# Two attention units of the last token tile are scored amid the last input columns, whose token halves are reordered

## The chip, the cores and the metric

The kernel runs on one core of one Trainium2 chip. The metric is the device time of one execution in microseconds (us), lower is better. The core has a matrix engine (PE; its weight loads are listed apart as PEld), a vector engine (DVE), a scalar engine (ACT), a general one (POOL), and queues that issue transfers between device memory (DRAM) and on-chip memory; nearly all transfers here are issued by the queue of SP. Each engine runs its own list of instructions in a fixed order and waits where an instruction's inputs, or the buffer it writes, are not ready. PSUM is the small memory that PE writes, in eight banks of 128 x 512 f32 numbers.

## The reference

One layer of a hybrid decoder, for a prompt of 1024 tokens and for 8 sample tokens of one step each:

```
h    = rms_norm(x) ;  p = h @ w_in                  # 1024 -> 3480 columns
q, rows4, rows_w, gates = NSA part of p             # 8 query heads, 2 key/value heads, width 64
o_nsa = gates . (compressed, causal/selected, window-of-512 attention)
o_rw  = RWKV-7 recurrence on the u columns of p
o_mem = attention of 4 more query heads over 256 memory tokens, keys and values from mem @ w_mem_kv
y = x + concat(o_nsa*silu(z_nsa), o_rw*silu(z_rw), o_mem*silu(z_mem)) @ w_out
```

With 1024 tokens there are 16 selectable blocks, and 16 are selected, so for the prompt the "selected" branch is causal attention over all earlier keys. The sample tokens run the same layer against cached pages. All rows, states and memory keys and values are returned too.

## The kernel before, in words

**Precision.** Products run on PE in a 4-byte format that keeps part of the mantissa, so an operand x is split into a high part (ACT copies it with rounding) and a low part (DVE or POOL subtracts), and a product is three matmuls: high·high, low·high, high·low. For the attention scores a 64-wide query is laid with its low part in the other 64 rows ("qhl", turned by PE into `p_q` and copied to `qs`), and the keys exist as `kh` and `kl`.

**Phase 1** (`phase1`) normalises x, transposes it into tiles `h` (high and low, 16 for each half of the tokens; H = 0 holds tokens 0 to 511 and the samples, H = 1 tokens 512 to 1023) in the pool `hp`, and walks over `w_in` in blocks of 128 columns. For a block, `wblock` loads 512 KB (`wraw`, SP), ACT makes `whi` and DVE `wlo`; `project` emits 24 matmuls per piece of tokens into `p_pr`: two pieces of 264 and 256 for H = 0, one of 512 for H = 1; a `do_...` function then evicts. For the gate columns `do_z` runs tanh on ACT and a multiply on DVE into the tile `zt`, and SP writes it to the DRAM buffer `z_d`. The RWKV recurrence is interleaved with the first 17 column blocks. The last four blocks (`cols[EARLY:]`, all gate columns) are emitted by `columns`: block by block, H = 0, then H = 1. While they run, a background generator `ahead` is stepped, `BG` steps for every 8 steps of the projection: it makes the compressed keys (`prompt_cmp`), the memory keys and values (`mem_kv`, matmuls into `p_mo`), the stacked keys (`attn_keys`, `p_k`), and the queries of tile 7 (`q_stack(7)`).

**Phase 2** (`phase2`) runs attention by tiles of 128 tokens, from tile 7 down to 0, in units of (tile, key/value head, pair of query heads), four to a tile. Of a unit, `attn_scores` makes four score blocks: PE writes `p_s` (two banks), DVE adds the mask, finds the minimum and evicts to `p`, ACT takes the exponential (L1357), POOL scales `p` by the gate and the inverse sum (L1382). `attn_turn` transposes `p` by PE into `p_pT` in groups of four 128 x 128 pieces, which ACT and DVE copy to `pt` in turn, and `attn_out` multiplies with the values into `p_o` and then with the gate columns in `cat`, which `load_z` reads back from `z_d`. The class `InOrder` holds PE to the written order. Side tasks are drawn by `slot` between these pieces: `query_tasks` brings the compressed branch of a tile (`attn_cmp`: scores `p_sc`, softmax `pcq`, four transposes) and the queries of the next (`q_stack(6)`: load `q` from the DRAM buffer `q_d`, ACT and POOL make `qhl`, PE transposes it to `p_q`), and other generators the sample tokens' and memory work. `until(0, ("cmp", i))` runs steps of `query_tasks` until tile i's compressed branch stands. The phase begins with six pieces of the scores of units 0 and 1, a slot after each.

**Order.** A tile of a pool reuses the memory of an earlier one, and the scheduler makes its first writer wait for the earlier one's last user. Pools of phase 2 lie over memory of phase 1. That is how a transfer of phase 2 can have to wait for an eviction of phase 1.

**Phase 3** projects `cat` by `w_out`, adds x, and finishes the sample tokens.

Of the kernel before, what the change touches and what calls it, by code (L numbers as in the profile page):

```python
# [10 lines left out]
F32 = mybir.dt.float32  # L11
# [10 lines left out]
NS = 8  # L22
# [3 lines left out]
PTB = 8  # L26
KB = 2
FREE = 0
ORDER = [4, 1, 11, 2, 3, 6, 5, 7, 13, 17, 10, 9, 15, 8, 0, 12, 14, 18, 16, 19, 20]
EARLY = 17  # L30
BG = 6
STEP = 0.7
# [16 lines left out]
def bc(ap, shape):  # L49
    return ap.to_broadcast(shape)  # L50
# [64 lines left out]
class Step:  # L115
# [130 lines left out]
    def h_tiles(self, H, k):  # L246
        W = HALF + (NS if H == 0 else 0)
        return [self.hp.tile([128, W], F32R, name=f"h{p}{H}_{k}") for p in range(2)]

# [201 lines left out]
    def phase1(self):  # L451
# [8 lines left out]
        with ExitStack() as ctx:  # L460
            P = lambda name, bufs, **k: ctx.enter_context(tc.tile_pool(name=name, bufs=bufs, reuse_waits="tile", **k))
            self.small = P("small", 2)
            self.hp = P("hp", 1)
            self.ev = P("ev", 1)
            self.wr = P("wr", 2)
            self.wp = P("wp", 2)
            rctx = ctx.enter_context(ExitStack())
            PR = lambda name, bufs: rctx.enter_context(tc.tile_pool(name=name, bufs=bufs, reuse_waits="tile"))
# [7 lines left out]
            self.ptr = P("ptr", 2, space=PSUM)  # L476
            self.pw = P("pw", 3, space=PSUM)
            self.hi, self.lo = ([], []), ([], [])
# [131 lines left out]
    def columns(self, tiles):  # L610

        rest = None
        for c0, do, j in tiles:
            m = 24 if j is None else 128
            hi, lo = self.wblock(c0, m)
            for H in range(2):
                out = []
                self.open = True
                for k, n in enumerate(self.project(H, hi, lo, m, out)):
                    if k < 7:  # L620
                        yield n
# [459 lines left out]
    def mem_kv(self):  # L1081
# [15 lines left out]
        for k in range(0, 8, 2):  # L1097
            raw = self.wr.tile([128, 2, 512], F32, name="wraw")
            nc.sync.dma_start(raw[:], I["w_mem_kv"][0, k * 128:(k + 2) * 128, :].rearrange("(k p) c -> p k c", p=128))
            wh = self.wp.tile([128, 2, 512], F32R, name="whi")  # L1100
            wl = self.wp.tile([128, 2, 512], F32R, name="wlo")
            A.activation(wh[:], raw[:], AF.Copy)
            V.tensor_tensor(wl[:], raw[:], wh[:].bitcast(F32), op=OP.subtract)
            yield
            for j in range(2):
                for t in range(2):
                    cs = slice(t * 128, (t + 1) * 128)
                    h, l = his[k // 4][:, (k + j) % 4, cs], los[k // 4][:, (k + j) % 4, cs]
# [4 lines left out]
        for t in range(2):  # L1113
            d0 = bass.AP(tensor=dst.tensor, offset=dst.offset + t * 128 * 512, ap=[[512, 128], [1, 512]])
            mv = self.slot(2 + t, [128, 256], F32, f"mv{t}")
            A.activation(mv[:], po[t][:, 256:512], AF.Copy)
            kn = self.norm_rope(po[t][:, 0:256].rearrange("p (t c) -> p t c", t=1), 5, 1, 4, None)
            nc.sync.dma_start(d0[:, 0:256], kn.rearrange("p h d -> p (h d)"))
            nc.sync.dma_start(d0[:, 256:512], mv[:])
            yield  # L1120

# [151 lines left out]
    def attn_cmp(self, i):  # L1273

        nc = self.nc
        V, A, G, PE = nc.vector, nc.scalar, nc.gpsimd, self.te
# [6 lines left out]
        for j in range(4):  # L1283
# [3 lines left out]
            if j == 1:  # L1287
                yield 0.1
        pcq = self.we.tile([128, 8, 64], F32, name="pcq", tag="pcq")
        v3 = lambda x: x.rearrange("p a b c -> p (a b) c")  # L1290
# [12 lines left out]
        V.tensor_tensor(gh, gh, gate[:, :, 0].rearrange("p (g h) -> p g h", g=2), op=OP.mult)  # L1303
        (G if i < 7 else V).tensor_tensor(pcq[:], pcq[:], bc(rc[:, :, None], [128, 8, 64]), op=OP.mult)
        yield 7.0 if i < 7 else 4.0
        self.pcT[i] = self.pt_copy(lambda j: pcq[:, 2 * j:2 * j + 2, :].rearrange("p a b -> p (a b)"), "c")
        yield

# [23 lines left out]
    def attn_scores(self, i, g, hp, Ps):  # L1332
# [28 lines left out]
        for b in range(2):  # L1361
# [3 lines left out]
            if split:  # L1365
                for h in range(2):
                    ps = self.pS.tile([128, 1024], F32, name="p_s", tag="s")
# [101 lines left out]
    def query_tasks(self):  # L1469

        yield from self.attn_cmp(7)
        self.done.add(("cmp", 7))
# [39 lines left out]
    def phase2(self):  # L1512
        tc, nc, I, O = self.tc, self.nc, self.I, self.O
        with ExitStack() as ctx:
            P = lambda name, bufs, **k: ctx.enter_context(tc.tile_pool(name=name, bufs=bufs, reuse_waits="tile", **k))
            self.small = P("small2", 2)
            self.we = P("we", 1)
            self.wk = P("wk", 1)
            self.tk = self.wk
# [3 lines left out]
            self.pM = Tag(self.pT, "t")  # L1523
            self.pp = P("pp", 4)
            self.load_z(7)
# [9 lines left out]
            P = [{} for _ in units]  # L1535
            self.done, self.tail, self.jobs, self.unit = set(), [], [], 0
# [96 lines left out]
    def sample_tables(self):  # L1633
# [11 lines left out]
        V.tensor_scalar(t[:, 4:7, :, 0], t[:, 4:7, :, 0], -1.0, None, op0=OP.mult)  # L1645
        return rows[:NS, 0:896].rearrange("p (k c) -> p k c", k=7)

    def sample_setup(self):
# [11 lines left out]
        for x in (qb, q64, qmb, self.gr):  # L1660
            G.memset(x[:], 0.0)
        sums = self.slot(1, [128, 1024], F32, "s_in1")[:, 0:128]
        nc.sync.dma_start(sums, I["c_rw"][:, 128:256])
        rows = self.sample_tables()

# [768 lines left out]
```

## Time and profile before

| What | us |
|---|---|
| three timed executions | 963.06, 966.33, 966.30 (median 966.3) |
| the profiled execution, its own time | 963.45 |
| its span (what the profile covers) | 961.7 |
| PE busy in the span | 923.5 (96%) |
| DVE, ACT, POOL busy | 653.2, 442.0, 179.5 |
| TensorE clock granted, mean | 0.998 |

Phase 1 ends, as PE sees it, with the last `p_pr` at 513.25 us; the compressed keys, memory keys and last columns fill about 436 to 513. Phase 2 starts behind it. In the timelines a row is a run of like instructions with the start, the duration, the line, the engine, output and inputs, and in brackets how long the engine stood idle before it and what ended that. In a table of stretches each engine's busy time stands with its number of instructions, then the granted clock (1.00 is full speed), the DMA engines' busy share and GB/s.

### The profile page before, as it was taken

The numbers are of one execution on the slowest core, as the hardware profiler recorded it, in microseconds if no ns is written. First come the engines' busy times: TensorE is split into PE (matmuls) and PEld (weight loads), VectorE is DVE, ScalarE is ACT, GpSimd is POOL, SyncE is SP. The second block draws the span as 40 slices with busy tenths as digits, with TensorE's granted clock in tenths as the row PEclk, the third lists the DMA queues.
The fourth block names the chain that finished last, engine by engine and source line by source line (L and its number), as shares of the span: only waits on it lengthen the run. The fifth ranks groups of instructions, "written<-read, shape, count | busy, mean of one in ns | idle before, by whom it ended". The sixth has DMA issues, their size and how long they took to land.

```text
span 961.7 us, 24727 instructions
## 1 busy us (share of the span) xinstructions
PE 923.5 (96%) x9845; PEld 785.5 (82%) x9845; DVE 653.2 (68%) x2025; ACT 442.0 (46%) x990; POOL 179.5 (19%) x270
## 2 busy tenths in 40 slices
PE   8999999999999998999998899999999998999997
PEld 8998888868898886788976787888888887887975
DVE  6668579846593798653447876756678996548474
ACT  7664324332432342222434666566576766324321
POOL 2000000000000000000001444354354665102010
PEclk9999999999999999999999999999999999999999
DMA  7521304312331127145426624240210035977721
GB/s 272 132 67 35 100 14 131 89 47 56 88 100 37 35 54 193 46 105 151 107 88 183 184 68 151 76 140 24 69 40 9 9 111 164 333 246 212 235 74 40
DMA packets 133964, 103.82 MB, mean 108 GB/s; under 512 B 34705, under 2 KB 121240, under 8 KB 133720
## 3 DMA queue, kind: packets, MB, share of 16 engines
q1 hardware_dynamic: 128888, 90.53, 32.5%
q0 software_dynamic: 3200, 10.49, 3.1%
q8 instruction: 78, 1.28, 0.5%
q10 hardware_dynamic: 1760, 1.21, 0.4%
q14 instruction: 38, 0.31, 0.1%
HBM read 83.61 MB, written 22.78 MB: 111 GB/s over the span
## 4 chain that ended last, share of the span: by engine, by line
PE 70%; DVE 16%; ACT 6%; DMA 4%; issue 3%; SPq 1%; POOL 0%; DVEq 0%; ACTq 0%; POOLq 0%
PE p_pr L87 20%; PE p_out L87 9%; PE p_pr L307 6%; PE p_s L87 5%; PE p_pT L87 4%; PE p_o L87 4%; PE p_hid L87 3%; ACT p L1357 2%; DVE p L1356 2%; PE p_iy L87 2%; PE p_z L87 1%; PE p_it L87 1%; PE p_sc L87 1%; DVE pt L1329 1%; DVE wlo L284 1%
## 5 line engine op out<-in xcount | busy, mean ns | idle before, releaser
L87 PE MATMUL p_pr<-h,whi 128*128 128x512 f32 (+5 forms) x1024 | 248.4, 335 | 0.0
L87 PEld LDWEIGHTS p_pr<-h,whi 128*128 128x128 f32 (+1 forms) x1024 | 161.8, 184 | 18.9 <-issue 2.8
L87 PE MATMUL p_pr<-h,wlo 128*128 128x512 f32 (+5 forms) x512 | 164.7, 325 | 0.6 <-DVE wlo L284 0.6
L1382 POOL TENSOR_SCALAR p<-p,fac,gates 128x640 f32<-128x640 f32 (+7 forms) x128 | 104.2, 825 | 106.1 <-DVE fac L1379 62.2
L1357 ACT ACTIVATE p<-p,nm 128x640 f32<-128x640 f32 (+7 forms) x128 | 93.0, 728 | 54.1 <-DVE nm L1356 47.6
L87 PEld LDWEIGHTS p_pr<-h,wlo 128*128 128x128 f32 (+1 forms) x512 | 93.6, 184 | 10.4 <-DVE wlo L284 0.8
L87 PE MATMUL p_pT<-ident,p 128*128 128x128 f32 x528 | 70.8, 279 | 5.7 <-ACT pt L1327 2.2
L1031 POOL MEMSET w2d<- 128x128 f32 x1 | 0.2, 206 | 393.6 <-PE p_yy L87 393.6
L1356 DVE CUSTOM_DVE_ANT_0 p<-p_s,bmask 128x512 f32<-128x512 f32 (+7 forms) x96 | 60.3, 662 | 18.4 <-PE p_s L87 16.6
L87 PEld LDWEIGHTS p_pT<-ident,p 128*128 128x128 f32 x528 | 56.7, 140 | 16.6 <-issue 6.4
L87 PE MATMUL p_s<-kh,qs 128*128 128x512 f32 (+3 forms) x191 | 66.3, 359 | 2.8 <-DVE nm L1356 2.8
L307 PE MATMUL p_pr<-h,whi 128*128 128x264 f32 (+2 forms) x320 | 68.6, 309 | 0.3 <-ACT whi L283 0.3
L87 PE MATMUL p_o<-pt,vs 128*64 128x128 f32 x1056 | 67.9, 277 | 0.4 <-DVE cat L1415 0.4
L284 DVE TENSOR_TENSOR wlo<-wraw,whi 128x1024 fp32r<-128x1024 f32 (+1 forms) x34 | 40.7, 1197 | 38.1 <-ACT whi L283 38.1
L87 PEld LDWEIGHTS p_o<-pt,vs 128*64 128x64 f32 x1056 | 57.0, 137 | 7.2 <-issue 3.8
L87 PE MATMUL p_s<-kl,qs 128*128 128x512 f32 (+3 forms) x192 | 61.0, 338 | 0.0
L283 ACT ACTIVATE whi<-wraw 128x1024 fp32r<-128x1024 f32 (+1 forms) x35 | 36.4, 1039 | 50.0 <-PE p_pr L87 35.7
L1329 DVE COPY pt<-p_pT 128x512 f32<-128x512 f32 (+1 forms) x72 | 48.3, 674 | 13.6 <-PE p_pT L87 12.8
L307 PEld LDWEIGHTS p_pr<-h,whi 128*128 128x128 f32 x320 | 51.1, 189 | 3.3 <-ACT whi L283 0.8
L87 PE MATMUL p_out<-woh,chi 128*128 128x512 f32 x128 | 51.7, 404 | 0.0
L87 PE MATMUL p_out<-woh,clo 128*128 128x512 f32 x128 | 50.2, 392 | 0.4 <-DVE clo L2267 0.4
L87 PE MATMUL p_out<-wol,chi 128*128 128x512 f32 x128 | 49.9, 390 | 0.0
(549 smaller groups left out, 1931.2 us busy)
## 6 DMA issues: line engine op xcount, KB each, us to landing
wraw<-in_w_in_dram SPq DMA_DIRECT2D x34, 512.0 KB, 4.0
pg<-in_c_pool_dram SPq DMA_DIRECT2D x32, 256.0 KB, 6.5
pg<-in_c_pool_dram SPq DMA_DIRECT2D x48, 128.0 KB, 2.2
x<-in_x_prompt_dram SPq DMA_DIRECT2D x8, 512.0 KB, 7.3
z_d<-zt SPq DMA_DIRECT2D x16, 256.0 KB, 2.2
cat<-z_d SPq DMA_DIRECT2D x8, 512.0 KB, 5.9
xres<-in_x_prompt_dram POOLq DMA_DIRECT2D x16, 256.0 KB, 3.9
out_dram<-xres POOLq DMA_DIRECT2D x16, 256.0 KB, 3.6
```

What stands on the lines that cost most here:

```text
L87: self.last = getattr(self.engine, op)(*a, **k)
L283: nc.scalar.activation(hi[:, :, :n], raw[:, :, :n], AF.Copy)
L284: (low or nc.vector).tensor_tensor(lo[:, :, :n], raw[:, :, :n], hi[:, :, :n].bitcast(F32), op=OP.subtract)
L307: self.last_mm = self.pe.matmul(ps[:m, :b - a], w[:, k, :m], h[k][:, a:b], start=(k == 0 and i == 0), stop=(k == 7 and i == 2))
L1031: nc.gpsimd.memset(w2d[:], 0.0)
L1329: nc.vector.tensor_copy(pt[:, :n], ps[:, :n])
L1356: V.tensor_tensor_reduce(halves(x), halves(ps), m, -1.0, 3.0e38, op0=OP.add, op1=OP.min, accum_out=nm[:, h, b:b + 1])
L1357: A.activation(x, x, AF.Exp, scale=-1.0, bias=nm[:, h, b:b + 1], accum_out=sm[:, h, b:b + 1])
L1382: nc.gpsimd.tensor_scalar(x, x, f[:, h, b:b + 1], gate[:, hd + h, 1 + b:2 + b], op0=OP.mult, op1=OP.mult)
```

## The change

Four things are moved, and no matmul is added or taken away.

1. `halves` takes the place of `columns` for the last four blocks: all four for H = 0, then all four for H = 1. Each block's weights are loaded and split once for each half, so four loads of 512 KB, four `whi` and four `wlo` are added. The eviction follows its projection at once. `BG` is 9 instead of 6.
2. When the four of H = 0 are through, the `h` tiles of half 0 (their pool is now a separate one, `hp0`), the three PSUM banks `pw`, and the pool `wk1` are freed. Over the first is laid the pool `pp` of the probabilities `p`, which before was opened in phase 2; two of the banks become `p7`, one score buffer. The background generator then goes on to `scores`, which emits `attn_scores` of the first two units of tile 7 amid the columns of H = 1. Phase 2 starts without scores of its own for these units, with two slots instead of six.
3. The compressed branch of tile 7 is split: its scores and softmax (`cmp_weights`) go into the background work of phase 1 (`stacked`), and the four transposes (`cmp_turn`) stay at the start of phase 2. Its last multiply is on POOL; before it was on DVE for tile 7. The constant tables of the sample tokens go into phase 1 too.
4. `mem_kv` copies both halves of `p_mo` to one tile, normalises the keys of both together and writes them with one transfer, where before each half had its own chain and two writes.

```diff
@@ phase1
-            self.hp = P("hp", 1)
+            hp1 = P("hp1", 1)
...
+            self.hp = hctx.enter_context(tc.tile_pool(name="hp0", ...)), hp1
...
-            self.wk = self.tk = P("wk1", 1)
+            self.wk = self.tk = wctx.enter_context(tc.tile_pool(name="wk1", bufs=1, reuse_waits="tile"))
             self.pM = Tag(self.ptr, "tr")
-            bg = self.ahead()
-            late = self.columns(cols[EARLY:])
+            def scores():
+                while len(self.half) < len(cols[EARLY:]):
+                    yield
+                pctx.close()
+                wctx.close()
+                hctx.close()
+                self.p7 = P("p7", 1, space=PSUM)
+                self.pp = self.kctx.enter_context(tc.tile_pool(name="pp", bufs=4, reuse_waits="tile", side="right"))
+                for n in range(UNITS):
+                    yield from self.attn_scores(7, 0, n, self.begun[n])
+                self.p7 = None
+
+            self.begun, self.half = [{} for _ in range(UNITS)], []
+            bg = chain(self.ahead(), scores())
+            late = self.halves(cols[EARLY:])
             for _ in group(late, 8):
                 for _ in islice(bg, BG):
                     pass
@@ ahead
+        def stacked():
+            while 7 not in self.qs:
+                yield
+            self.pc7 = self.slot(3, [128, 8, 64], F32, "pcq")
+            yield from self.cmp_weights(7, self.pc7)
+            self.tables = self.sample_tables()
-        yield from weave(chain(self.prompt_cmp(), self.mem_kv()), keys())
+        yield from weave(chain(self.prompt_cmp(), stacked(), self.mem_kv()), keys())
+    def halves(self, tiles):
+        for H in range(2):
+            for c0, do, j in tiles:
+                out = []
+                yield from self.project(H, *self.wblock(c0, 128), 128, out)
+                do(H, out, j)
+                self.half.append(H)
@@ mem_kv
+        m = self.slot(6, [128, 2, 512], F32, "mrows")
+        for t in range(2):
+            A.activation(m[:, t], po[t][:], AF.Copy)
...
@@ query_tasks
-        yield from self.attn_cmp(7)
+        yield from self.cmp_turn(7, self.pc7)
@@ phase2
+            self.wk = P("wk", 1)
             self.we = P("we", 1)
-            self.wk = P("wk", 1)
...
-            self.pp = P("pp", 4)
...
-            start = chain(scores(0), scores(1))
-            for k in range(6):
-                next(start)
+            start = chain(*(scores(n) for n in range(UNITS, 2)))
+            for k in range(2):
+                next(start, None)
                 slot()
```

**PE, amid the columns.** In the lists below a row is a line, an operation, output and inputs, and the shape; `kh` and `kl` are the keys, `qs` the queries. PE in the kernel before, at the end of the last column:

```order
L307 MATMUL p_pr<-h_7_913,whi 128x512
L307 MATMUL p_pr<-h_7_914,whi 128x512
L307 MATMUL p_pr<-h_7_913,wlo 128x512
L84 MATMUL p_s<-kh_6300,qs 128x512
L87 MATMUL p_s<-kl_6301,qs 128x512
L87 MATMUL p_s<-kh_6303,qs 128x512
L87 MATMUL p_s<-kl_6304,qs 128x512
L87 MATMUL p_sc<-cmask 128x512
```

PE in the changed kernel, in the second half's columns (line numbers are higher by one for the same helper):

```order
L308 MATMUL p_pr<-h_1_674,whi 128x512
L1395 MATMUL p_s<-kh_6303,qs 128x128
L1396 MATMUL p_s<-kl_6304,qs 128x128
L1395 MATMUL p_s<-kh_6306,qs 128x512
L1396 MATMUL p_s<-kl_6307,qs 128x512
L308 MATMUL p_pr<-h_1_673,wlo 128x512
```

The scores that followed the last column, all of them in a row, stand in groups of four between projections.

**PE, where the queries of tile 6 are turned.** Before, in the first part of phase 2:

```order
L87 MATMUL p_sn<-ident,s_in_7259 128x8 x7
L87 MATMUL p_pT<-ident,pcq 128x128 x4
L87 MATMUL p_s<-kh_6300,qs 128x128
L87 MATMUL p_s<-kl_6301,qs 128x128
L87 MATMUL p_s<-kh_6303,qs 128x512
L87 MATMUL p_s<-kl_6304,qs 128x512
L87 MATMUL p_q<-ident,qhl 128x128 x4
```

Now, at the border of the two phases (the last `p_pr` of all is the third row):

```order
L308 MATMUL p_pr<-h_7_916,whi 128x512
L308 MATMUL p_pr<-h_7_917,whi 128x512
L308 MATMUL p_pr<-h_7_916,wlo 128x512
L88 MATMUL p_pT<-ident,p 128x128 x8
L88 MATMUL p_q<-ident,qhl 128x128 x4
L88 MATMUL p_pT<-ident,p 128x128 x10
L88 MATMUL p_s<-kh_6303,qs 128x512
```

Before, 53 rows lay between the last `p_pr` and the first `p_q` of tile 6; now one row of eight transposes does.

**SP, the load of those queries.** The queue's order before:

```order
L1118 DMA out_dram<-nr_y 128x256
L320 DMA z_d<-zt 128x512
L1129 DMA kd<-out_dram 128x4x64
L1254 DMA q<-q_d 128x768
L1129 DMA kd<-out_dram 128x4x64
L1254 DMA q<-q_d 128x768
```

and now:

```order
L1171 DMA mv<-out_dram 128x256
L321 DMA z_d<-zt 128x512
L1824 DMA mxv_8132<-in_cache_mem_dram 128x2x256 x2
L321 DMA z_d<-zt 128x512
L1295 DMA q<-q_d 128x768 x2
L1311 DMA y_rw<-y_d 128x256
L1312 DMA cat_7335<-z_d 128x8x128
```

The last `z_d` row is the write of the very last column's gates in both. The loads of `q` stand right behind it now. The memory of the first `q` tile lies over the `zt` tile that this write reads, so the load also waits until the write has landed.

More of the change, by code (lines that the diff above doesn't have):

```diff
@@ L27 @@
 KB = 2
+UNITS = 2
 FREE = 0
@@ L30 @@
 EARLY = 17
-BG = 6
+BG = 9
 STEP = 0.7
@@ L247, in h_tiles @@
         W = HALF + (NS if H == 0 else 0)
-        return [self.hp.tile([128, W], F32R, name=f"h{p}{H}_{k}") for p in range(2)]
+        return [self.hp[H].tile([128, W], F32R, name=f"h{p}{H}_{k}") for p in range(2)]
     def turn_hs(self):
@@ L466, in phase1 @@
             self.wp = P("wp", 2)
+            hctx = ctx.enter_context(ExitStack())
+            self.hp = hctx.enter_context(tc.tile_pool(name="hp0", bufs=1, reuse_waits="tile")), hp1
             rctx = ctx.enter_context(ExitStack())
@@ L476, in phase1 @@
             self.ptr = P("ptr", 2, space=PSUM)
-            self.pw = P("pw", 3, space=PSUM)
+            pctx = ctx.enter_context(ExitStack())
+            self.pw = pctx.enter_context(tc.tile_pool(name="pw", bufs=3, reuse_waits="tile", space=PSUM))
             self.hi, self.lo = ([], []), ([], [])
@@ L555, in phase1 @@
             self.key_pools()
-            self.wk = self.tk = P("wk1", 1)
+            wctx = ctx.enter_context(ExitStack())
+            self.wk = self.tk = wctx.enter_context(tc.tile_pool(name="wk1", bufs=1, reuse_waits="tile"))
             self.pM = Tag(self.ptr, "tr")
-            bg = self.ahead()
-            late = self.columns(cols[EARLY:])
+            def scores():
[12 more added lines that the diff above has]
+            late = self.halves(cols[EARLY:])
             for _ in group(late, 8):
@@ L1111, in mem_kv @@
             yield
-        dst = O["mem_kv_prompt"]
[L1113 to L1120, printed above, removed]
+        m = self.slot(6, [128, 2, 512], F32, "mrows")
+        for t in range(2):
+            A.activation(m[:, t], po[t][:], AF.Copy)
+        y = m[:, :, 0:256].rearrange("p t (h d) -> p t h d", d=64)
+        sq = self.slot(7, [128, 8, 64], F32, "nr_sq")
+        A.activation(sq[:].rearrange("p (t h) d -> p t h d", t=2), y, AF.Square)
+        ss = self.small.tile([128, 8], F32, name="nr_ss", tag="nrss8")
+        V.tensor_reduce(ss[:], sq[:], axis=AX.X, op=OP.add)
+        r = self.rsqrt(self.small, ss[:], 8, 1.0 / 64, 1e-6)
+        yield
+        V.tensor_tensor(y, y, bc(r.rearrange("p (t h) -> p t h", t=2)[:, :, :, None], [128, 2, 4, 64]), op=OP.mult)
+        V.tensor_tensor(y, y, bc(self.gains[:, 5:6, None, :], [128, 2, 4, 64]), op=OP.mult)
+        dst = O["mem_kv_prompt"]
+        nc.sync.dma_start(bass.AP(tensor=dst.tensor, offset=dst.offset, ap=[[512, 128], [128 * 512, 2], [1, 512]]), m[:])
+        yield
     def mem_keys(self):
@@ L1273, in attn_cmp, with cmp_turn, cmp_weights @@
     def attn_cmp(self, i):
+        pcq = self.we.tile([128, 8, 64], F32, name="pcq", tag="pcq")
+        yield from self.cmp_weights(i, pcq)
+        yield 7.0
+        yield from self.cmp_turn(i, pcq)
+    def cmp_turn(self, i, pcq):
+        self.pcT[i] = self.pt_copy(lambda j: pcq[:, 2 * j:2 * j + 2, :].rearrange("p a b -> p (a b)"), "c")
+        yield
+    def cmp_weights(self, i, pcq):
         nc = self.nc
@@ L1288, in attn_cmp @@
                 yield 0.1
-        pcq = self.we.tile([128, 8, 64], F32, name="pcq", tag="pcq")
         v3 = lambda x: x.rearrange("p a b c -> p (a b) c")
@@ L1303, in attn_cmp @@
         V.tensor_tensor(gh, gh, gate[:, :, 0].rearrange("p (g h) -> p g h", g=2), op=OP.mult)
[L1304 to L1307, printed above, removed]
+        G.tensor_tensor(pcq[:], pcq[:], bc(rc[:, :, None], [128, 8, 64]), op=OP.mult)
     def attn_rwkv(self, i):
@@ L1366, in attn_scores @@
                 for h in range(2):
-                    ps = self.pS.tile([128, 1024], F32, name="p_s", tag="s")
+                    ps = (self.p7 or self.pS).tile([128, 1024], F32, name="p_s", tag="s")
                     scores(ps[:, c0:512], qs[:, hd + h, :], b, c0, 512)
@@ L1534, in phase2 @@
                 groups += [(n, a, min(a + size, total)) for a in range(0, total, size)]
-            P = [{} for _ in units]
+            P = self.begun + [{} for _ in units[UNITS:]]
             self.done, self.tail, self.jobs, self.unit = set(), [], [], 0
@@ L1645, in sample_tables @@
         V.tensor_scalar(t[:, 4:7, :, 0], t[:, 4:7, :, 0], -1.0, None, op0=OP.mult)
-        return rows[:NS, 0:896].rearrange("p (k c) -> p k c", k=7)
+        self.nc.sync.dma_start(rows[:, 896:1024], self.I["c_rw"][:, 128:256])
+        return rows[:NS, 0:896].rearrange("p (k c) -> p k c", k=7), rows[:, 896:1024]
     def sample_setup(self):
@@ L1661, in sample_setup @@
             G.memset(x[:], 0.0)
-        sums = self.slot(1, [128, 1024], F32, "s_in1")[:, 0:128]
-        nc.sync.dma_start(sums, I["c_rw"][:, 128:256])
-        rows = self.sample_tables()
+        rows, sums = self.tables
         x, sq, xr = (self.we.tile([128, 8, NS], F32, name=f"s_x{k}") for k in range(3))
```

## The prediction

> **What bounds the kernel now.** I read the page's busy shares and chain first, then tables of stretches around the end of phase 1, PE's waits there, and the timelines of each engine.
>
> ```profile
> PE 923.5 (96%) x9845; PEld 785.5 (82%) x9845; DVE 653.2 (68%) x2025; ACT 442.0 (46%) x990; POOL 179.5 (19%) x270
> PE 70%; DVE 16%; ACT 6%; DMA 4%; issue 3%; SPq 1%; POOL 0%; DVEq 0%; ACTq 0%; POOLq 0%
> ```
>
> PE is busy for 923.5 of 961.7 us, and it holds 70% of the chain that ended last. The change gives PE the same work, so the time can move only through PE's idle time, 38.2 us in all, and through the clock. The stretches that the change touches:
>
> ```profile
> 436.00:513.00 77.00, 75.29 (x484) 64.12 (x483) 32.86 (x92) 29.67 (x60) 3.26 (x6) 1.00 0.40 111
> 513.00:540.00 27.00, 21.35 (x147) 17.04 (x145) 23.56 (x76) 15.64 (x33) 10.87 (x11) 0.94 0.82 241
> 540.00:600.00 60.00, 57.07 (x582) 47.45 (x581) 39.85 (x105) 40.62 (x100) 26.12 (x30) 1.00 0.35 110
> ```
>
> (Columns: stretch, length, then busy time of PE, PEld, DVE, ACT, POOL, the granted clock, DMA share, GB/s.) The last columns leave PE idle for 77.00 - 75.29 = 1.7 us, the border of the phases for 27.00 - 21.35 = 5.65 us, the 60 us behind it for 2.9 us. Inside the border:
>
> ```profile
> 517.50:520.00 2.50, 0.01 (x1) 0.01 (x1) 2.06 (x5) 0.03 (x1) 0.00 (x0) 1.00 0.45 95
> 520.00:522.00 2.00, 2.00 (x7) 1.38 (x8) 2.00 (x4) 1.26 (x3) 0.00 (x0) 0.62 0.98 298
> 522.00:524.50 2.50, 2.30 (x6) 1.22 (x5) 1.39 (x7) 2.50 (x6) 1.35 (x2) 0.62 1.05 345
> 530.00:532.10 2.10, 0.00 (x0) 0.02 (x1) 2.10 (x6) 1.07 (x3) 1.91 (x3) 1.00 0.84 261
> ...
> 519.99 0.33 PE L87 MATMUL p_s<-kh,qs 128*128 128x128 f32 x1 [2.55 <-DVE nm L1356]
> 526.33 1.89 PE L87 MATMUL p_pT<-ident,p 128*128 128x128 f32 x15 [0.47 <-POOL p L1382]
> 532.11 0.63 PE L87 MATMUL p_pT<-ident,pcq 128*128 128x128 f32 x4 [2.38 <-DVE pcq L1304]
> ```
>
> Two waits hold nearly all of it: 2.55 us for the first score eviction, 2.38 us for the compressed softmax's multiply. Behind the first the granted clock is 0.62 for 4.5 us, a loss of 4.5 x 0.38 = 1.7 us; behind the second it stays at 1.00. So the border costs 5.65 + 1.7 = 7.35 us over PE's work, and with the columns' 1.7 the part that the change can touch is **9.05 us**.
>
> **The change part by part.** *Scores amid the columns.* They remove the 2.55 us wait: DVE's four evictions a unit now run beside projections.
>
> ```profile
> 518.71 1.22 DVE L1356 CUSTOM_DVE_ANT_0 p<-p_s,bmask 128x1024 f32<-128x1024 f32 x1
> 521.60 0.82 DVE L1356 CUSTOM_DVE_ANT_1 p<-p_s,bmask 128x640 f32<-128x640 f32 x1
> 513.25 0.39 PE L307 MATMUL p_pr<-h,wlo 128*128 128x512 f32 x1
> 511.85 0.39 PE L307 MATMUL p_pr<-h,wlo 128*128 128x512 f32 x1
> ```
>
> Two units are 4 x 1.22 + 4 x 0.82 = 8.2 us of DVE. The two rows of `p_pr` lie six matmuls apart, 0.233 us each, so a column of 24 lasts 5.6 us, and DVE is busy for 32.86 of 77 us there: the evictions fit, though with one score buffer instead of two a group that comes too early waits. I count 0.35 us for it.
>
> *The compressed softmax in phase 1.* This removes the 2.38 us wait; its multiply has tens of us of columns over it, on POOL instead of DVE. *Doubled weights.*
>
> ```profile
> L284 DVE TENSOR_TENSOR wlo<-wraw,whi 128x1024 fp32r<-128x1024 f32 (+1 forms) x34 | 40.7, 1197 | 38.1 <-ACT whi L283 38.1
> L283 ACT ACTIVATE whi<-wraw 128x1024 fp32r<-128x1024 f32 (+1 forms) x35 | 36.4, 1039 | 50.0 <-PE p_pr L87 35.7
> wraw<-in_w_in_dram SPq DMA_DIRECT2D x34, 512.0 KB, 4.0
> ```
>
> Four more splits are 4.8 us of DVE and 4.2 us of ACT, against 44 and 47 us in which they are free between 436 and 513; a load's 4.0 us lies under a column's 5.6. The cover is that the load goes out a column ahead. Where it is thin, between the memory keys' weights and the first column behind them, I count 0.65 us. *BG 9* draws the keys' work faster, so PE meets its makers sooner:
>
> ```profile
> PE p_k L1199 <- DMA kd<-k_d: 0.7, 2, 0.5
> PE p_k L1147 <- POOL kd L1140: 0.6, 1, 0.6
> PE p_pT L87 <- ACT pt L1327: 1.2, 2, 0.6
> ```
>
> The waits for `kd` I leave at about their size, 0.3 and 0.7; `p_sc` now stands close behind the compressed keys' own copies and I give it 0.95, two or three copies of 0.3 to 0.4 us; and the first `p_s` needs banks that the copies of `p_mo` (two of ACT's 128x512, 0.60 each by the row of `zt` below) must leave: 0.75. Sum for the columns: 0.3 + 0.7 + 0.95 + 0.65 + 0.75 + 0.35 = **3.7 us** instead of 1.7. All hang on distances in the order alone; half of the four that are new hidden gives 2.3, half as much again 5.1. The norm of the memory keys in one piece has the columns over it: nothing.
>
> *The queries of tile 6.* This is the term that decides. `p_q` now stands eight transposes behind the last `p_pr`, and `q` can be loaded only when the last column's `z_d` write has landed. Before:
>
> ```profile
> 513.68 0.60 ACT L318 ACTIVATE zt<-p_pr 128x512 f32<-128x512 f32 x1 [1.39 <-PE p_pr L307]
> 514.56 0.67 DVE L319 SCALAR_TENSOR_TENSOR zt<-zt,p_pr 128x512 f32<-128x512 f32 x1
> 515.26 0.33 SPq L320 DMA_DIRECT2D z_d<-zt  x1
> z_d<-zt SPq DMA_DIRECT2D x10, 256.0 KB, 2.2
> 518.28 0.50 SPq L1254 DMA_DIRECT2D q<-q_d  x1
> 521.95 0.42 ACT L1259 ACTIVATE qhl<-q 128x256 fp32r<-128x256 f32 x1 [0.74 <-DMA q<-q_d]
> 522.45 0.74 POOL L1260 TENSOR_TENSOR qhl<-q,qhl 128x256 fp32r<-128x256 f32 x1 [19.62 <-ACT qhl L1259]
> 533.27 0.60 PE L87 MATMUL p_q<-ident,qhl 128*128 128x128 f32 x4
> ```
>
> The last `p_pr` ended at 513.25 + 0.39 = 513.6 and `qhl` stood at 523.2, 9.6 us later; PE had other work and asked at 533.27. Now, from the end of the last `p_pr`: tanh 0.6; on DVE a copy of `pt` first and then the gate, together to 2.0; the write lands 2.2 later, at 4.2; `q` takes 521.95 - 518.28 = 3.67, to 7.9; ACT 0.42 and POOL 0.74 make it 9.05. PE fills about 1.0 of that with eight transposes (15 take 1.89 above). Ten transposes, the next scores and all of phase 2 are queued behind `p_q` on PE, so PE stands for about **8.1 us**. If `q` lands as fast as the nearest quiet row, `z_d`'s 2.2, it is 6.6; if the two loads that leave together cost half a us each way more, 9. I take 8.1, `q`'s own row. The clock then falls as it did after 2.55 us idle, and I count the same 1.7.
>
> [...]
>
> *Sum:* (3.7 + 8.1 + 1.7) - 9.05 = **+4.45 us**. The behind-lying 60 us I leave as they are. On the profiled execution's 963.45 that is 967.9. The median of the three timed executions, 966.3, lies 2.85 above the profiled one, and one of them, 963.06, below it; I add half, 1.5, and round to **969.5 us**.
>
> **The rivals.** *Slower still: the clock stays low longer.* After the stall PE meets 4 `p_q` and 10 `p_pT` first (0.60 and 1.29 us in the rows before), where before it met wide matmuls. If transposes do not lift the clock, these 1.9 us run at 0.62 first, 3.0 us for 1.9, and the 4.5 us come after them: 1.2 us more, +5.65; with 9 us of stall +6.5, and 970 to 972 on my scale. For it: no row here shows a rise out of transposes. Against it: the 15 `p_pT` at 526.33 ran at 1.00, though the clock had risen before them. [...]
>
> *About as before: the stall repays itself.* While PE stands for 8 us, DVE, ACT and POOL work off what they owe, and the evictions of two units are done already. In the 60 us behind the border PE lost 2.9 us; before, DVE was busy for 23.56 of the border's 27 us, which speaks for a backlog. If all 2.9 go, it is +1.55; with `q` at 2.2, +0.05: 965 to 967.5. Against it: DVE is at 39.85 of 60 there, so the backlog was short.
>
> *Faster: DVE paced the border, and `q` comes early.* Let S be the stall. The sum is S - 3.65, less up to 2.9 from behind. It turns negative for S below 3.65, or below 6.6 if all 2.9 go and the lead of two units holds. The place is `p_q`, and the price at S = 1 (`q` ready as PE arrives, 8 us sooner than I work out) is -2.65 - 2.9 = -5.5, and without a stall no clock loss either, -7.2: 956 to 962. For it: the two removed waits and the lost clock are 6.6 us, all of which it keeps. Against it: two transfers in a row stand between the last column and `p_q`, and even at 2.2 us each they leave 6.6.
>
> **How the numbers follow.** The forecast (+2.5 to +6) has 0.55, the low clock (up to +8) 0.12, the repaid stall (0 to +2.5) 0.21, faster 0.12, at 956 to 963. What a measurement of this kernel can tell from no change is about 0.5%, 4.8 us. The forecast's +4.45 lies a little under that bound, so nearly half of its chance and nearly all of the low clock's are slower: 0.27 + 0.12 = 0.39, with a little of the rest 0.40. Faster by more than 4.8 us is most of the last rival: 0.10. That leaves 0.50 for within 0.5%. The range, 962.5 to 975, reaches from the upper end of the faster case to the low clock on top of the upper timed execution; the forecast's own is 966 to 972.
>
> **What would show it.** Right: one idle stretch of 7 to 9 us in front of `p_q`, put down to `qhl` or `q`, about 1 us behind the last `p_pr`, the clock at about 0.6 behind it; the waits for `nm` and `pcq` gone; evictions of `p_s` inside the columns, with PE idle there for 2.3 to 5.1 us. Wrong: `q` issued before the last `z_d`, or a stall under 5 us; PE idle in the columns for more than 6 us, most likely at `p_s` or `wlo`; or less idle time than 1.5 us in the 60 us behind.

## The result

The changed kernel is slower: 973.38 us in the median of eight executions (966.62 to 977.5) against 962.9 of the kernel before (eight, 960.51 to 966.33); the ratio is 1.0085, 95% interval 1.0061 to 1.011. Twice more, beside other kernels, it came to 1.0069 (1.0044 to 1.0095) and 1.0053 (1.0036 to 1.007). The profiled execution took 967.89 us, 4.44 more than the profiled one before; its span is 966.1.

The page of the changed kernel, engine totals and chain, then the stretches that answer to the columns, the border and what is behind it, with the border's idle part and the 3.3 us behind it on rows of their own:

```profile
PE 924.6 (96%) x9845; PEld 785.6 (81%) x9845; DVE 658.7 (68%) x2013; ACT 445.2 (46%) x993; POOL 180.4 (19%) x271
PE 68%; DVE 16%; DMA 6%; ACT 6%; issue 3%; SPq 1%; POOL 0%; DVEq 0%; ACTq 0%; POOLq 0%
...
436.00:528.40 92.40, 87.40 (x549) 73.29 (x547) 52.33 (x128) 42.96 (x83) 12.92 (x14) 1.00 0.48 138
528.40:545.00 16.60, 9.20 (x73) 8.16 (x72) 5.16 (x10) 6.98 (x16) 3.56 (x5) 0.79 0.81 249
545.00:610.00 65.00, 63.13 (x634) 53.24 (x634) 47.87 (x128) 42.40 (x101) 28.05 (x34) 1.00 0.28 90
529.00:535.70 6.70, 0.00 (x0) 0.00 (x0) 0.30 (x1) 1.46 (x7) 1.24 (x3) 0.74 0.57 185
535.70:539.00 3.30, 3.24 (x15) 3.24 (x16) 0.69 (x1) 1.28 (x3) 1.42 (x3) 0.50 1.08 303
```

PE's idle time is 966.1 - 924.6 = 41.5 us, 3.3 more than before, and DMA has 6% of the chain instead of 4%. For 6.7 us at the border PE does nothing at all. The rows of PE, SP, ACT and POOL there, in that order, from the timelines, and the transfer as the chain of waits has it:

```profile
527.14 0.39 PE L308 MATMUL p_pr<-h,wlo 128*128 128x512 f32 x1
527.38 1.03 PE L88 MATMUL p_pT<-ident,p 128*128 128x128 f32 x8
535.76 1.12 PE L88 MATMUL p_q<-ident,qhl 128*128 128x128 f32 x4 [7.35 <-POOL qhl L1301]
...
529.32 0.33 SPq L321 DMA_DIRECT2D z_d<-zt  x1
531.41 0.80 SPq L1295 DMA_DIRECT2D q<-q_d  x2
534.48 0.72 ACT L1300 ACTIVATE qhl<-q 128x256 fp32r<-128x256 f32 x2 [2.32 <-DMA q<-q_d]
534.98 1.41 POOL L1301 TENSOR_TENSOR qhl<-q,qhl 128x256 fp32r<-128x256 f32 x2 [3.01 <-ACT qhl L1300]
...
531.41 3.06 DMA q<-q_d
```

This is the chain of the prediction, link by link: the last projection, the gate's write, the load of `q` that waits for it, the split, and PE standing 7.35 us in front of `p_q`. The waits for `pcq` and for the first score at the phase's start are gone.

### The profile page after: what moved, and what is told of

It reads as the page before. It is cut to its first block, busy times and chain, and to the rows that moved or that the text cites. A ratio compares the mean times of both kernels' runs of the same rounds, so it can differ in the third digit from the quotient of the medians.

```text
span 966.1 us, 24725 instructions
## 1 busy us (share of the span) xinstructions
PE 924.6 (96%) x9845; PEld 785.6 (81%) x9845; DVE 658.7 (68%) x2013; ACT 445.2 (46%) x993; POOL 180.4 (19%) x271
## 4 chain that ended last, share of the span: by engine, by line
PE 68%; DVE 16%; DMA 6%; ACT 6%; issue 3%; SPq 1%; POOL 0%; DVEq 0%; ACTq 0%; POOLq 0%
PE p_pr L88 20%; PE p_out L88 7%; PE p_pr L308 7%; PE p_s L88 4%; PE p_pT L88 4%; PE p_o L88 4%; ACT p L1406 3%; PE p_hid L88 3%; DVE p L1405 2%; PE p_iy L88 2%; DMA pg<-in_c_pool_dram 2%; PE p_z L88 1%; PE p_it L88 1%; DVE pt L1378 1%; PE p_sc L88 1%
## 5 line engine op out<-in xcount | busy, mean ns | idle before, releaser
L285 DVE TENSOR_TENSOR wlo<-wraw,whi 128x1024 fp32r<-128x1024 f32 (+1 forms) x38 | 45.9, 1208 | 42.8 <-ACT whi L284 42.8
L284 ACT ACTIVATE whi<-wraw 128x1024 fp32r<-128x1024 f32 (+1 forms) x39 | 40.6, 1041 | 54.2 <-PE p_pr L88 36.8
L88 PE MATMUL p_s<-kh,qs 128*128 128x512 f32 (+3 forms) x176 | 59.6, 351 | 0.0
L88 PE MATMUL p_s<-kl,qs 128*128 128x512 f32 (+3 forms) x176 | 54.4, 330 | 0.0
L1376 ACT ACTIVATE pt<-p_pT 128x512 f32<-128x512 f32 (+1 forms) x72 | 41.5, 581 | 19.3 <-PE p_pT L88 16.3
```

Of the source, the lines that this page charges most:

```text
L88: self.last = getattr(self.engine, op)(*a, **k)
L284: nc.scalar.activation(hi[:, :, :n], raw[:, :, :n], AF.Copy)
L285: (low or nc.vector).tensor_tensor(lo[:, :, :n], raw[:, :, :n], hi[:, :, :n].bitcast(F32), op=OP.subtract)
L1376: nc.scalar.activation(pt[:, :n], ps[:, :n], AF.Copy)
```

## The experiments

Twelve runs were made; e1 and e12 are the changed kernel itself. The "kernel before" of each ratio ran beside it on the same chip. A profile's PE time is split below into idle time and busy time; since PE's instructions are the same in all but e3 and e4, whose idle time is partly filled with added work, a higher busy time is mostly time at the low clock: e12, below, has 6.1 us more of it than the first profile of the same program, beside 13.7 us more at a clock of 0.50.

| Kernel | median us (n) | ratio to before (95%) | profiled: span, PE busy, idle |
|---|---|---|---|
| before | 962.9 (8) | | 961.7, 923.5, 38.2 |
| changed | 973.38 (8) | 1.0085 (1.0061 to 1.011) | 966.1, 924.6, 41.5 |
| e1 same | 969.37 (7) | 1.0069 (1.0044 to 1.0095) | 967.1, 926.7, 40.4 |
| e2 queries early | 963.09 (10) | 0.9987 (0.9968 to 1.0007) | 959.7, 924.7, 35.0 |
| e3 matmuls in the stall | 968.92 (10) | 1.0054 (1.0031 to 1.0077) | 973.6, 936.9, 36.7 |
| e4 transposes in the stall | 970.84 (4) | 1.0073 (1.0045 to 1.01) | 968.3, 934.5, 33.8 |
| e5 queries early, BG 8 | 961.63 (10) | 0.9981 (0.996 to 1.0003) | 959.9, 925.4, 34.5 |
| e6 queries early, spread | 959.18 (5) | 0.9925 (0.9898 to 0.9952) | 959.0, 923.7, 35.3 |
| e7 queries early, no units | 969.32 (10) | 1.0046 (1.0027 to 1.0066) | 967.1, 928.8, 38.3 |
| e8 queries turned later | 965.54 (10) | 1.0008 (0.9989 to 1.0028) | 961.9, 925.5, 36.4 |
| e9 early, spread, BG 12 | 958.64 (6) | 0.9947 (0.9931 to 0.9964) | 953.8, 924.0, 29.8 |
| e10 spread alone | 965.64 (10) | 1.0014 (0.9998 to 1.003) | 961.0, 923.7, 37.3 |
| e11 halves alone | 965.13 (10) | 1.0017 (1.0004 to 1.003) | 961.8, 923.4, 38.4 |
| e12 same | 969.45 (6) | 1.0053 (1.0036 to 1.007) | 970.1, 930.7, 39.4 |

### What the stall costs: e2 and e8

e2 puts the queries of tile 6 into a buffer that is free during the columns:

```diff
+        if i == 6:
+            q = self.slot(5, [128, 12, 64], F32, "q6")
...
-            pool, tag, nb = (self.kt, "kd4", KB) if first else (self.we, "qhl", 2)
+            pool, tag, nb = (self.kt, "kd4", KB) if first or (i == 6 and b == 0) else (self.we, "qhl", 2)
```

> The queries of tile 6 are loaded into a cat buffer that is free during the columns and their first third is split in the keys' pool, so that neither load nor split waits for the last write of z_d; PE's order stays the same row for row there. Theory A: the wait in front of p_q goes from 7.35 us to under 0.7, the clock behind it stays at 1.00 and the second group of executions vanishes: 967.9 - 7.35 - 1.65 = 959 us, 958 to 962, 0.996 of the kernel before. Theory B (the stall only stood where other waits would have stood, since the engines behind work off their debt in it): PE waits for pt, nm or p instead, 4 us or more come back, and it takes 963 to 968; if the second group is caused elsewhere, there are still executions 6 us above the others.

Measured beside e1, which is the changed kernel itself: 963.09 against 969.37 us, 6.3 less, 0.9987 of the kernel before against 1.0069. PE's rows at the place, and the table of stretches of e2:

```profile
528.59 1.04 PE L88 MATMUL p_pT<-ident,p 128*128 128x128 f32 x8
529.46 0.60 PE L88 MATMUL p_q<-ident,qhl 128*128 128x128 f32 x4
...
528.00:545.00 17.00, 15.03 (x139) 12.45 (x138) 11.62 (x32) 10.72 (x25) 5.50 (x7) 1.00 0.81 234
477.00:484.00 7.00, 6.44 (x21) 4.85 (x21) 4.21 (x11) 2.41 (x5) 0.00 (x0) 0.51 0.44 117
```

No wait is left in front of `p_q`, the clock at the border is 1.00, and PE is idle for 2 us there. So the stall is a cause of the slowdown: without it the change is no slower than the kernel before. It is not the only one, as e10 below shows. And 959 (958 to 962) was expected of theory A, and 963 came, in the range of theory B, though none of the waits of theory B stand in the profile. Part of the difference stands in the last row: a stretch of 7 us at a clock of 0.51 in the columns, which the first profile of the changed kernel and that of the kernel before do not have.

e8 leaves the load where it is and draws the transposes later:

```diff
         self.done.add(("cmp", 7))
+        yield 10.0
```

> The changed kernel with its loads as they are, but the transposes of tile 6's queries are drawn 10 us of PE work later (a yield in query_tasks ahead of them), so that PE does units 0 and 1 of tile 7 while the queries come. Theory A: the wait in front of p_q falls from 7.35 to under 1 us and the time is that of e2, 960 to 965, since PE has some 12 us of transposes, scores and products that don't need the queries. Theory B (these wait for evictions or cat in turn): 964 to 969.

965.54 us, 1.0008 of the kernel before, a little over the range given for theory A and inside that of theory B, 964 to 969. PE's row for `p_q`:

```profile
542.89 0.63 PE L88 MATMUL p_q<-ident,qhl 128*128 128x128 f32 x4
```

No wait stands in front of it here either: PE has other work until then. The longest wait at the border is 0.94 us, for an operand of the sample tokens. So two ways, one that moves the load and one that moves the transposes, both bring the time back to that of the kernel before, and both leave the doubled weight loads and the new PSUM buffer in place. What these two cost by themselves is not separated by e2 and e8.

### The clock: e1, e3, e4 and e12

> The changed kernel itself, unaltered, beside the three others on one chip. Its timed executions so far fell into two groups, 966.6 to 967.9 us at a mean granted clock of 0.996 and 973.1 to 977.5 at 0.984 to 0.989; the profiled one was of the first group. Theory A (the stall of 7.35 us in front of p_q, and a clock that stays low for longer behind it in most executions): again 966 to 978 with both groups, and a profile of the second group would show the clock at about 0.5 for some 12 us more, behind that stall. Theory B (the second group's loss lies elsewhere: the doubled weight loads, the columns): a profile of the second group shows the low clock in another place, or more idle time of PE.

e1 took 967.71 to 974.27, in two groups again. Its profile, of an execution at 968.83, has the clock at about 0.5 behind the stall, and also near 480 us, where the first profile of the same program had 1.00. To fill the stall, e3 and e4 put work that nobody needs ahead of `p_q`:

```diff
+            if i == 6 and b == 0:
+                c = PE.clock
+                for _ in range(28):
+                    PE.matmul(ps[:].rearrange("p a b -> p (a b)"), self.qs[7][:, 0, :], self.kh[0][:, 0, :], start=True, stop=True)
+                PE.clock = c
```

(e4: 60 times `PE.transpose(ps[:, n % 4, :], self.ident[:], self.ident[:])` instead.)

> The stall stays, but 28 matmuls of 128x512 whose result is overwritten stand in front of p_q, 28 x 0.233 = 6.5 us of PE work that nobody needs. Theory A with the clock: PE is idle for under 1 us at once there, the clock stays at 1.00, and every execution takes 967.9 - 1.65 = 966.2 us, 965 to 968; none at 973. If the second group's loss has nothing to do with the idle stretch: 966 to 978 in two groups, as without the matmuls.

> As with the matmuls, but 60 transposes of 128x128, about 60 x 0.11 = 6.6 us. If transposes count as work for the clock: 965 to 968 in every execution, clock 1.00 behind them. [...]

PE's timeline of e3 and then of e4, with one row of e4's table of stretches:

```profile
531.55 6.62 PE L88 MATMUL p_q<-kh,qs 128*128 128x512 f32 x28
539.22 0.66 PE L88 MATMUL p_q<-ident,qhl 128*128 128x128 f32 x4 [1.05 <-POOL qhl L1301]
```

```profile
531.56 6.71 PE L88 MATMUL p_q<-ident 128*128 128x128 f32 x60
539.09 0.66 PE L88 MATMUL p_q<-ident,qhl 128*128 128x128 f32 x4 [0.82 <-POOL qhl L1301]
...
536.00:538.00 2.00, 2.00 (x20) 2.00 (x19) 0.00 (x0) 0.19 (x1) 0.00 (x0) 1.00 0.92 315
```

Both keep the clock at 1.00 through the former stall; the 60 transposes take 6.71 / 60 = 112 ns each to the end. So these 60 transposes left the clock at 1.00, as the 28 matmuls did (1.00 from 528.40 to 545.00 us in both). The times hardly move, though (968.92 and 970.84 against 969.37): both lie above the 965 to 968 that was expected if the clock at the stall made the difference, and e3 still had executions at 972 to 976. The low clock behind the stall is therefore not what parts the groups, and what it costs by itself, 1.65 us by the profile, is too little to be told from these medians.

e12, once more the changed kernel, gave a profile of an execution at 971.85 us:

> The changed kernel unaltered, beside e9 to e11 on one chip: 966 to 978 in two groups. A profile of an execution above 972 us would show where the second group loses: low clock behind the stall for longer (theory A), or near 478 us and in other places that have nothing to do with the stall, as the profile of e3 at 975 us had it.

Its stretches at a low clock, roughly cut to their extent:

```profile
478.70:482.00 3.30, 3.07 (x8) 2.36 (x9) 1.57 (x6) 0.71 (x3) 0.00 (x0) 0.50 0.75 212
533.00:540.20 7.20, 4.05 (x17) 3.86 (x18) 1.12 (x2) 2.22 (x5) 2.14 (x3) 0.53 0.99 285
730.70:738.00 7.30, 7.30 (x36) 6.07 (x37) 3.25 (x10) 2.04 (x5) 0.87 (x2) 0.54 0.01 2
820.00:823.50 3.50, 3.50 (x24) 2.84 (x22) 0.31 (x2) 1.05 (x2) 1.79 (x4) 0.52 0.94 253
```

Four of them instead of the first profile's one. PE's busy time is 930.7 - 924.6 = 6.1 us higher for the same work. So the longer executions of one and the same program, as far as profiles show them, are those in which the clock falls in more places, and only one of the places is the stall. The mean granted clock that was recorded with every execution says the same: of the first eight it was 0.996 in the three up to 967.9 us, and 0.984 to 0.989 in the five from 973.1 us on. Theory A's clock part falls with this. e3's profile, at 975.38 us, shows the same picture with low stretches from 478.6, 734.6 and 823.4 us and none at the border.

The trace also holds a record of the granted clock, and by it the four stretches of e12 last 3.41, 6.83, 6.83 and 3.41 us, at 0.50. In all 14 profiles the clock is either 1.00 or 0.50, every low stretch that ends within the span lasts one, two or three times 3.413 us, and each begins a whole number of such steps after the clock first rose. In the kernel before one of 3.413 us begins at 520.46 us, 150 steps after the rise at 8.47; in the first profile of the changed kernel one of 6.827 us begins at 532.18, 154 steps after the rise at 6.53. Where these steps lie against the kernel's work differs from execution to execution: the first rise comes between 5.9 and 8.5 us after the start of the span in the 14 profiles.

### The columns: e5, e6, e10, e9

What stands ahead of the low stretch near 478 us, the timeline of PE in e1 shows: narrow `p_sc` matmuls (here the last of 16) between two waits. The last three rows are of the changed kernel's first profile: the same two waits, and the new wait for a weight block.

```profile
475.58 0.33 PE L1188 MATMUL p_k<-ident,kd 128*128 128x128 f32 x1 [0.62 <-POOL kd L1181]
478.19 0.28 PE L1339 MATMUL p_sc<-ckl,qs 128*128 128x64 f32 x1
479.30 0.80 PE L1145 MATMUL p_mo<-whi,mhi 128*128 128x512 f32 x1 [0.56 <-ACT mhi L1128]
475.55 0.33 PE L1188 MATMUL p_k<-ident,kd 128*128 128x128 f32 x1 [0.63 <-POOL kd L1181]
479.27 0.50 PE L1145 MATMUL p_mo<-whi,mhi 128*128 128x512 f32 x1 [0.56 <-ACT mhi L1128]
500.63 0.72 PE L308 MATMUL p_pr<-h,whi 128*128 128x512 f32 x2 [1.25 <-ACT whi L284]
```

The first profile had the same work and the same waits at this place, and the clock at 1.00. What the records show to differ is where the steps of 3.413 us fall. In the six profiles with the low clock here, the step that ends where it falls holds 12 to 16 of the 16 `p_sc` and a part of a wait. In the two that have the same order and no low clock (the first profile and e8), the end of a step parts the 16, and no step holds more than 11. Eight profiles agree with this; no run moved the steps on purpose.

In the kernel before, `p_sc` stood in phase 2, and projections stood between the memory rows' transposes and their products. e5 sets BG = 8 in e2; e6 takes smaller steps in e2:

```diff
-            if j == 1:
+            if j == 1 or i == 7:
                 yield 0.1
```

> The kernel with the early queries (e2), with BG = 8 instead of 9. In e2's profile the granted clock is about 0.5 from 477 to 484 us, behind 16 narrow p_sc matmuls and two waits of 0.6 us that stand together; that stretch is at 1.00 in the kernel before and falls in e1 to e4, all four. With BG = 8 more projections stand between these pieces. If the packed background is what lowers the clock there: no low stretch in the columns, the wait for mhi gone, and 963.1 - 3 = 960 us in the median, 957 to 961.5, under the kernel before by 0.3 to 0.7%. If it is chance, or bound to the place: 961 to 965, as e2, with the low stretch again.

> The kernel with the early queries (e2) at BG = 9, with a step after each pair of heads in tile 7's compressed scores, so that the background goes on in smaller pieces and projections come between the transposes of the memory rows and their products. If waits and narrow work packed together lower the clock: none or a shorter low stretch near 478 us, 957 to 962. If BG itself matters (how early the rest comes): as e2, 961 to 965.

e5: 961.63 us, 0.9981 (0.996 to 1.0003), which is not told apart from e2 or from the kernel before; three of its ten executions lie at 965.8 to 966.6, so they still spread. e6: 959.18 us, 0.9925 in five executions, clear of noise faster than the kernel before. In both profiles the stretch near 478 is at 1.00 and the wait for `mhi` is gone. e10 has e6's step without the early queries:

> The changed kernel with the smaller pieces alone; the queries load late as in it. What is removed is the low clock near 478 us, not the stall. If the stall alone makes the kernel slower than before: about 7 us above e6, 965 to 969, with the 7 us in front of p_q or a little less, since a wait of about 2.5 us for pt now stands in the same place. If the low clock near 478 us is what parts the two groups of executions: no execution above 971.

965.64 us, 1.0014, and no execution above 967.29 in ten, where the changed kernel had 10 of 21 above 971. PE's waits at the border, two rows of e10 and one of e6, and e6's table of stretches near 478:

```profile
527.05 1.09 PE L88 MATMUL p_pT<-ident,p 128*128 128x128 f32 x8 [2.46 <-ACT pt L1376]
531.83 1.12 PE L88 MATMUL p_q<-ident,qhl 128*128 128x128 f32 x4 [3.69 <-POOL qhl L1301]
529.30 1.58 PE L88 MATMUL p_pT<-ident,p 128*128 128x128 f32 x8 [2.46 <-ACT pt L1379]
```

```profile
474.00:478.00 4.00, 3.37 (x26) 3.01 (x25) 2.45 (x16) 0.66 (x2) 0.41 (x2) 1.00 0.11 36
478.00:482.00 4.00, 4.00 (x28) 3.60 (x28) 3.13 (x7) 1.81 (x3) 0.00 (x0) 1.00 0.22 14
```

So the stall and the packed background are two separate losses. e10 against e12 on the same chip is 965.64 against 969.45, 3.8 us. Of this 7.42 - 6.15 = 1.3 us can be the shorter waits at the border, 2.46 + 3.69 = 6.15 us in e10 against 7.42 in e12; the rest goes with the packing. What the stall costs is less certain. By the ratios of e10 and e6, 1.0014 and 0.9925 from two chips, it is about 8.5 us. But e6 has the same 2.46 us for `pt`, so e10 waits only 3.69 us more, and the two profiles differ by 961.0 - 959.0 = 2.0 us of span; e10's is of its fastest execution, e6's of its slowest. Of the eight profiles whose order has the packed piece, six show the clock low near 478 us (e1, e2, e3, e4, e7, e12); of e5, e6, e9 and e10, none. Why the executions above 971 vanish with it, although their other low stretches lie at 730 and 820 us, the runs don't say.

e9 joins the early queries, the smaller steps and BG = 12:

> The early queries (e2) and the smaller pieces (e6) with BG = 12, by which the scores of both units are done half a column before the end, as in the changed kernel, and projections stand between the two groups of transposes again. In e6 PE waits 2.46 us there for a copy of pt, with the clock at about 0.5 behind it for some 3 us. If that wait comes only of the order: it goes, the clock holds at 1.00 from the columns to 545 us, and the time is 959.2 - 2.5 - 1.6 = 955 us, 954 to 959. If something else must wait in its place (the keys' loads, met sooner at BG = 12): 958 to 963.

958.64 us, 0.9947 (0.9931 to 0.9964). Its profile has the least idle time of all, 29.8 us, and is at 953.8 us of span the shortest; the wait for `pt` is down to 0.36 us. The clock still falls once, to 0.50 from 534.1 to 537.5 us, behind a wait of 0.92 us for an operand of the sample tokens, so the hope that it would hold was wrong. e6 and e9 overlap in their intervals; both beat both kernels, by 0.5 to 0.75% the one before.

### What the scores amid the columns are worth, and the halves: e7 and e11

e7 is e2 with `UNITS = 0`.

> The kernel with the early queries (e2), but UNITS = 0: no score is made amid the columns, the first two units are scored at the start of the second phase again; halves, doubled loads, the early compressed softmax and the pools stay. Theory A (scores amid the columns are worth the first-eviction wait of 2.55 us and the 1.7 us of clock behind it, once no stall eats them): 3 to 6 us above e2, 966 to 969, with a wait for nm of about 2.5 us and the clock at 0.6 behind it. Theory B (the early softmax and queries make the gain, DVE's backlog costs nothing): within 2 us of e2.

969.32 us, 1.0046 against e2's 0.9987: some 6 us. The first transposes of `p` wait for the whole chain of eviction, exponential and scale:

```profile
526.85 0.47 PE L88 MATMUL p_pT<-ident,p 128*128 128x128 f32 x1 [4.20 <-POOL p L1434]
526.80:533.00 6.20, 5.44 (x23) 4.85 (x24) 1.57 (x3) 1.20 (x2) 1.87 (x2) 0.50 1.04 291
```

The wait I named, for `nm`, isn't it; it is 4.2 us for `p`, with the clock at 0.50 for 6.2 us behind. Scored amid the columns, two units are worth these 6 us in the changed kernel's order. That is not their worth against the kernel before: e7 keeps the two pieces at the start of phase 2, so the transposes are asked for after two score blocks, where the kernel before makes six pieces first and waited 2.55 us. With six pieces e7 could lose less; it wasn't run.

e11 is the kernel before with the columns in halves and nothing else (the last four columns by `halves` instead of `columns`).

> The kernel before with one part of the change: the last four columns all for the first half, then all for the second, so that four more weight blocks are loaded and split; BG = 6, scores and softmax as before. Theory A (the doubled blocks lie under the columns): within 2 us of the kernel before, waits for whi and wlo under 2 us in sum. Theory B (the doubled loads crowd the queue and the splits): 3 us or more slower, with those waits at 3 us.

965.13 us, 1.0017 (1.0004 to 1.003), 1.6 us, within theory A's bound. Waits for `whi` and `wlo` are small, 0.2 and 0.5 us, and both are for the weights of the memory keys, none for a doubled block. Yet the profile has one wait of 6.29 us for the first score's eviction, as the compressed softmax comes first on DVE there and itself waits for ACT:

```profile
523.66 0.44 PE L87 MATMUL p_s<-kh,qs 128*128 128x128 f32 x1 [6.29 <-DVE nm L1364]
521.69 0.69 DVE L1306 TENSOR_REDUCE c_s<-pcq 128x8 f32<-128x512 f32 x1 [2.66 <-ACT pcq L1304]
```

The idle time in the span is about that of the kernel before (38.4 us against 38.2): this wait takes the place of the 2.55 and 2.38 us waits.

## Why the prediction was right, and where it was off

**Bound.** Right: PE's work is the same, and everything went through its idle time and the clock.

**The queries of tile 6**, the term that was to decide: 8.1 us predicted (6.6 to 9), 7.35 measured. The end of the last `p_pr` is 527.53. The write went out 1.8 us later (2.0 predicted), `q` at 3.9 (4.2), ACT began at 6.95 (7.9), `p_q` at 8.2 (9.05). Most of the difference is the load, 3.07 us instead of 3.67. The DMA engines were busy for a share of 0.66 while it ran, and of 0.81 during the old one; whether the lighter load is the reason, no run tests. e2 and e8 show that the stall is a cause of the slowdown.

**The clock behind it**: 1.7 predicted, 3.3 us at 0.50 measured, 1.65. The 0.62 over 4.5 us that I took from the old profile was one step of 3.41 us at 0.50; in the changed kernel the clock is low for two steps, 532.2 to 539.0, of which the first passes in the stall. Right for the place; that this would be all was the step that failed, below.

**The columns**: 3.7 us predicted (2.3 to 5.1), 92.40 - 87.40 = 5.0 measured. That the sum came near is partly luck, since its parts are off both ways. The 0.95 for `p_sc` did not come at all, and the banks of the first `p_s` cost 0.2 where I gave 0.75. But `whi` alone took 1.25 where I gave 0.65 to both weight splits, and of PE's waits in the changed kernel these are larger than I had them, or new:

```profile
PE p_s L1395 <- DVE nm L1405: 1.1, 1, 1.1
PE p_mo L1145 <- ACT mhi L1128: 0.6, 1, 0.6
PE p_mo L1145 <- DVE wlo L1138: 0.5, 1, 0.5
```

The wait for the eviction ahead, which I put down to the one score buffer, took 1.1 us where I gave 0.35; `mhi` and the `wlo` of the memory keys I didn't have.

**The waits removed**: both gone, as said.

**Behind the border** I left the 60 us as they were. From 545 to 610 us PE was idle for 1.9 us, where the kernel before lost 65.00 - 62.24 = 2.8 in the same stretch of time, which holds nearly the same work:

```profile
545.00:610.00 65.00, 62.24 (x632) 51.89 (x631) 43.62 (x112) 42.77 (x104) 27.99 (x33) 1.00 0.33 105
```

So at most 0.9 us were repaid, not the 2.9 of that rival.

**The sum** for the profiled execution was +4.45, and +4.44 is what it took: 0.75 less at the stall and 0.9 less behind it are balanced by 1.3 more in the columns and other small differences. That the two agree so closely is luck, all the more as one profile shows one execution. **The time**, 973.4, lies 3.9 above the 969.5 forecast, inside the range of 962.5 to 975, but above the 966 to 972 that I gave the forecast itself. The ratio of 1.0085 means 8.2 us (5.9 to 10.6), nearly twice the 4.45; the two repeats gave 6.6 and 5.1. Slower by more than 0.5%, which came, had a chance of 0.40, less than the 0.50 for no change that could be told. The step that failed is the clock term, sized from one profiled execution with the clock low at a single place, in "I count the same 1.7". Executions of this program differ in how often the clock falls, by some 6 us of PE's time between two profiles, and the changed kernel packs narrow matmuls and short waits into the columns, while the two profiles of the earlier order (before and e11) show no low clock in the columns. This I had costed at nothing but waits. Adding half of the 2.85 us by which the old median lay above its profile was no help: eight executions put the median of the kernel before at 962.9, under its profile.

**The rivals.** *Slower still, the clock low for longer* was right in that low clock made it slower than the sum, wrong in the mechanism: here the transposes did not leave the clock low. Behind the stall it rose at 539 us, with little but four `p_q` and ten `p_pT` since PE went on, and e4 shows it at 1.00 through 60 of them. *The stall repays itself* did so by a third at most. *Faster* described the kernel without the stall: for S = 0 it gave -3.65 less the stretch behind and the clock; e2 came to -0.1%, and e6, without the packed piece, to -0.75% (0.48 to 1.02), 7.2 us by the ratio and 5.8 by the medians. That the packed piece took it back in e2 follows from their times alone: their two profiles differ by only 0.7 us of span.

So a gain of some 6 to 7 us was in the change, as e6 has it, and it went to one load that waits for the last write of the phase before, and to the packed work in the columns, behind which the clock falls in six of eight profiles.

## What to carry to other kernels

When work is moved ahead over a border, look at what the moved work used to cover: here it was the load of the next tile's queries, and the buffer that load shares with the last writer of the phase. Before a term is sized by a clock seen in one profile, look whether other executions of the same program have the same; a program whose times fall in groups is told by several profiles. In this kernel it paid to spread narrow matmuls and their waits among wide ones rather than to run them in one piece: e10 took 965.64 us where e12 took 969.45.

## What the hardware showed that was not expected

The clock fell without any long idle time. In e12 PE was busy for 3.10 of the 3.42 us ahead of the fall at 478.65, the first row below; the step of the second row, in which PE was busy for only 2.33 us, left the clock at 1.00. So in these traces the share of idle time doesn't decide by itself. At 731 us the fall came behind waits of 0.88 and 0.29 us and a run of 64-wide `p_sc` matmuls:

```profile
475.23:478.65 3.42, 3.10 (x22) 2.61 (x22) 1.93 (x3) 1.86 (x4) 0.00 (x0) 1.00 0.00 0
509.37:512.78 3.41, 2.33 (x11) 1.63 (x11) 3.38 (x6) 1.85 (x3) 2.99 (x2) 1.00 0.17 61
729.08 0.66 PE L88 MATMUL p_pT<-ident,p 128*128 128x128 f32 x4 [0.88 <-DVE pt L1378]
730.03 0.50 PE L88 MATMUL p_sc<-cmask 128*128 128x512 f32 x1 [0.29 <-ACT pt L1376]
```

Both places have narrow `p_sc` matmuls beside short waits. That these together lower the clock agrees with e5, e6, e9 and e10, which break up one of the two places and stand at 1.00 there, from 478.70 to 482.00 us; it wasn't tried by itself, by widening the matmuls with the waits left. They don't stand at every fall: where e12 has 0.52 from 820.00 to 823.50 us, the same program's first profile has no `p_sc` from 800 to 824 us, only waits such as 1.01 and 0.39 us that end at 814.72 and 816.68, and there the clock stays at 1.00. And the 60 transposes in a row of e4 kept the clock at 1.00, at 112 ns each.
